# Hybrid encoder layer on one core: three products turned from by-feature to by-token blocks of 512 columns, with their results turned through DRAM

## The chip, the cores and the metric

The kernel runs on one core of a Trainium2 chip. The metric is device time in microseconds (us) of one execution; the kernel before takes 2039.56 us, the median of three runs (2039.33 to 2039.59). Profiles come from one execution recorded by the hardware profiler. A core has TensorE (matrix products, PE in the views; its weight loads are PEld), VectorE (DVE), ScalarE (ACT), GpSimd (POOL) and SyncE (SP). Here SP and POOL mostly issue DMAs.

## The reference

One layer works on x of 256 tokens by 2048 features, in float32:

```python
h = rms_norm(x, ffn1_norm);  x = x + 0.5 * swiglu_ffn(h, ffn1_w_in, ffn1_w_out)
h = rms_norm(x, mix_norm)
a_val, a_gate, g_u, g_v = split(h @ w_mix_in)
ya = silu(layer_norm(causal_conv31(a_val * sigmoid(a_gate))))
yb = gelu(g_u) * (masked W_s @ layer_norm(gelu(g_v)) + b)
x = x + concat(rms_norm(ya), rms_norm(yb)) @ w_mix_out
q = rms_norm(x, xattn_norm) @ w_q;  k, v = split(rms_norm(mem, mem_norm) @ w_kv)
x = x + softmax(q k^T / sqrt(512)) v @ w_o          # 4 heads of 512 features
h = rms_norm(x, ffn2_norm);  x = x + 0.5 * swiglu_ffn(h, ffn2_w_in, ffn2_w_out)
return rms_norm(x, final_norm)
```

The feed-forward's hidden width is 5632, the memory has 256 tokens.

## The kernel before

**Precision.** Every operand of a product is kept as a high and a low half in TensorE's fp32r type, and a product is the sum of high x high, high x low and low x high. Weights come from DRAM as float32 in pieces of 512 KB, which `weights` (L134) loads on SP's queue, casts on ScalarE (high half, L141) and subtracts on VectorE (low half, L142). Four raw pieces (`wraw`) and three pieces of halves (`whl`) are held at a time.

**Two forms of a product.** `gemm_t` (L191, by way of `ahead` and `product_part`) works by feature: the weights of 128 features are TensorE's stationary operand, and x streams past, both halves of it at once for the weights' high half (512 columns, L171), x's high half alone for the weights' low half (256 columns, L179). The result has features on the partitions and tokens in the columns, as the next product wants it. `gemm_n` (L209) works by token: x's halves are the stationary operand, and 512 weight columns stream past in three matmuls per k and half of the tokens (L220, L221, L222). Its result has tokens on the partitions. `sent` (L356) turns such a result into the layout by feature: VectorE transposes it in squares of 32 (L359), POOL's queue writes it to DRAM (L361) and reads it back in four pieces (L364). The columns of the weights are laid out beforehand so that the squares land in order (`by_blocks`).

**Order of work.** The program is written for a builder that orders each engine's instructions by its own forecast of the timeline, within the data's dependences; `tc.issue_after` adds an edge. `beside` hands out small pieces of other work after each weight piece, `between` is a list of pieces that `gemm_n` takes one by one. The two feed-forwards are different: `Line` (L419) keeps a list of items, each with its weight piece, and fixes the order on every engine (L497). Item s may be followed by preparation of up to six items ahead at the start. Its buffers for halves (`places`) and raw weights (`raws`) are lists too.

**The stages around the change.** The mixers' stage (L1172) makes the conv and gMLP inputs, the memory's keys and values by token. Then come

- the mixers' output projection (L1448 to L1459): by feature, 16 blocks; the first three begin with their upper half of k, and each block ends in `residual` (L330): two VectorE adds into xT from PSUM (L333), the halves of the next normalized x (`gained`, L318, on ScalarE L320 and VectorE L321) and its squares (L291);
- the queries (L1470), by feature, four blocks a head, each joined, and split into halves;
- per head, `probabilities` (L1482: scores, softmax), `turned` (L1507: transposes on TensorE) and `attend` (L1521: four results of 128 features, each split into `o_hl`);
- attention's output projection (L1550 to L1583), by feature, with parts of its first blocks put between heads 2 and 3, and `residual` behind each block;
- the second `FeedForward` (L1586), built after that. Its `begin` (L817) has 16 items of one k each, with the turning of x for the last residual (`x_turn`, L1594, after items 1 to 8), its two stores (`x_leaves`, after items 6 and 10), its squares' sums, and the sums of halves for a seven-product scheme (`sides`, L618) after items 3, 6, 9 and 12.

PSUM has eight banks: six named acc, two named aux. Large SBUF areas S0, S1, S2 are passed from stage to stage.

Of the kernel before, what the change touches and what calls it, by code (L numbers as in the profile page):

```python
# [14 lines left out]
ALU = mybir.AluOpType  # L15
# [47 lines left out]

LAST = ((256, True, False), (512, True, False), (256, False, False), (512, False, False), (512, False, True))
# [30 lines left out]
def layer(ctx: ExitStack, tc: tile.TileContext, a: dict):  # L95
# [19 lines left out]
    newest = [None]  # L115

# [17 lines left out]
    def weights(src, kk, n, hl=None):  # L134
# [6 lines left out]
        nc.scalar.copy(out=hl[:, 0, :size], in_=raw[:, :size])  # L141
# [67 lines left out]
    def gemm_n(w, x_hl, per=0.0, between=None, after=4, acc=None, ks=None, step=2):  # L209

        acc = acc or [ps.tile([P, 2, 256], F32, name="acc").rearrange("p a b -> p (a b)") for _ in range(2)]
        nk = w.shape[1]
        for k0 in ks or range(0, nk, 2):
            kk = min(2, nk - k0)
            hi, lo = weights(w[:, k0:k0 + kk, :], kk, 512)
            for k in range(kk):
                x = x_hl(k0 + k)
                for t in range(2):
                    s = slice(t * P, (t + 1) * P)
                    nc.tensor.matmul(acc[t], lhsT=x[:, 0, s], rhs=hi[:, k], start=k0 + k == 0, stop=False)  # L220
                    nc.tensor.matmul(acc[t], lhsT=x[:, 0, s], rhs=lo[:, k], start=False, stop=False)  # L221
                    nc.tensor.matmul(acc[t], lhsT=x[:, 1, s], rhs=hi[:, k], start=False, stop=k0 + k == nk - 1)  # L222
# [107 lines left out]
    def residual(acc, f, scale, x_hl, norm, ss):  # L330
# [6 lines left out]
        square_into(ss, xT[:, f], f == 0)  # L337

# [187 lines left out]
    class FeedForward:  # L526
# [6 lines left out]
        def __init__(self, stack, tags, name, x_hl, gain, w_in, w_out, patterns, sums, steps, out_s, late):  # L533
# [25 lines left out]
            spare = big.tile([P, 8192], F32, name="spare", tag=tags[2])  # L559
            raws = [spare[:, i * 1024:(i + 1) * 1024] for i in range(6)]  # L560
            self.u = [spare[:, 6144 + i * 512:6144 + (i + 1) * 512] for i in range(4)]
            self.raws_summed = [raws.pop() for _ in range(2)]
# [8 lines left out]
            self.in_low, self.in_high = self.fixed(lows), self.fixed(highs)  # L571
            self.in_spare = self.fixed(raws)
            self.line.places.extend(self.in_ring + self.in_low + self.in_high)
# [243 lines left out]
        def begin(self, before, after, scales):  # L817
# [19 lines left out]
            for i in range(len(self.spairs)):  # L837
# [4 lines left out]
                for q, part in enumerate(parts):  # L842
                    items[3 * i + q + 3].post.append(part)
# [135 lines left out]
    with ExitStack() as stack:  # L979
# [3 lines left out]
        )  # L983
        line = ff.line
# [187 lines left out]
    with ExitStack() as stack:  # L1172
        with tc.tile_pool(name="mix", bufs=1) as pool:
# [274 lines left out]
            ws = [a["w_mix_out"][f] for f in range(3)]  # L1448
            accs = ahead(ws, lambda k: y_hl[:, k], per=1.3, ks=[(8, 8)], end=False)
# [4 lines left out]
            for f in range(KD):  # L1454
                if f < 3:
                    acc = gemm_t(a["w_mix_out"][f], lambda k: y_hl[:, k], acc=accs[f], ks=[(0, 8)])
                else:
                    acc = gemm_t(a["w_mix_out"][f], lambda k: y_hl[:, k])
                residual(acc, f, 1.0, x_hl, "xattn_norm", ss)  # L1459


        with tc.tile_pool(name="attn", bufs=1) as pool:
            o_hl = big.tile([P, KD, 2, T], F32R, name="o_hl", tag="S2")

            def query(q_hl, d, acc):
                t = ev.tile([P, T], F32, name="tg")
                joined(acc, t)
                split(q_hl[:, d, 0], q_hl[:, d, 1], t)

            def queries(h, between=None):  # L1470
                q_hl = pool.tile([P, KH, 2, T], F32R, name="q_hl", bufs=2)
                if h == 0:
                    accs = ahead([a["w_q"][d] for d in range(2)], lambda k: x_hl[:, k])
                    for d in range(2):
                        query(q_hl, d, accs[d])
                for d in range(2 if h == 0 else 0, KH):
                    query(q_hl, d, gemm_t(a["w_q"][h * KH + d], lambda k: x_hl[:, k]))
                    if d == KH - 2 and between is not None:
                        between()
                return q_hl  # L1480

# [393 lines left out]
```

## Time and profile before

| | us |
|---|---|
| median of three runs | 2039.56 |
| profiled execution | 2040.7 |
| its span, first to last instruction | 2038.5 |
| TensorE busy | 2027.2 |
| VectorE busy | 1796.6 |
| ScalarE busy | 1244.7 |
| mixers' output projection, on TensorE | from 1051.7 |
| first matmul of attention's output projection | 1245.7 |
| DMA moved | 488.50 MB |

A row of groups reads: line, engine, operation, output<-inputs, shapes, count, then busy time and mean duration. A row of a stretch (`A:B`) gives the length, then for PE, PEld, DVE, ACT and POOL the busy time with the number of instructions, then TensorE's granted clock, the busy share of the DMA engines and GB/s. A row of waits gives total, number and longest in us. In the view of one line or tile, durations are minimum/median/maximum in ns, followed by the first and the last start in us. Matmuls overlap, so a matmul's own duration says less than the spacing of starts.

### The profile page before, as it was taken

The page shows a single profiled execution, that of the slowest core. Times are in us where ns is not written, and L with a number is a line of the kernel's source. Part 1 is how long each engine was busy: PE and PEld are TensorE (multiplying, and loading weights), DVE is VectorE, ACT ScalarE, POOL GpSimd, SP SyncE. Part 2 cuts the span into 40 slices and gives each one's busy share as a digit, 9 for nine tenths or more (in the row PEclk, how much of TensorE's full clock was granted, in tenths as well). Part 3 has the DMA queues.
Part 4 walks back from the last instruction along what each step waited for, and adds up shares of the span by engine and source line. Part 5 has one row for each costly group of instructions (what it writes and reads, how often), then busy time and mean ns, then how long its engine had stood idle before and what let it go on. Part 6 is the DMA issues. An engine that isn't in the chain of part 4 may idle for free.

```text
span 2038.5 us, 26768 instructions
## 1 busy us (share of the span) xinstructions
PE 2027.2 (99%) x9388; PEld 1690.5 (83%) x9388; DVE 1796.6 (88%) x2538; ACT 1244.7 (61%) x1609; POOL 123.6 (6%) x180
## 2 busy tenths in 40 slices
PE   9999999999999999999999999999999999999998
PEld 7888888888888887888888899888888888888886
DVE  7999999989898979999897666788999999988997
ACT  7666666656665654545675455556667666655555
POOL 0000000000110011011000000000001000000002
PEclk9999999999999999999999999999999999999999
DMA  9889898989676577677665543687888898896665
GB/s 352 272 259 275 269 277 260 273 250 289 213 262 233 194 260 224 210 227 230 203 196 195 186 157 116 204 290 259 262 263 268 269 276 268 233 300 203 207 226 177
DMA packets 146071, 488.50 MB, mean 240 GB/s; under 512 B 17040, under 2 KB 28944, under 8 KB 145296
## 3 DMA queue, kind: packets, MB, share of 16 engines
q1 hardware_dynamic: 130032, 432.64, 62.2%
q0 software_dynamic: 15328, 53.49, 13.1%
q8 instruction: 73, 1.20, 0.2%
q10 hardware_dynamic: 576, 0.66, 0.1%
q14 instruction: 62, 0.51, 0.1%
HBM read 465.76 MB, written 20.97 MB: 239 GB/s over the span
## 4 chain that ended last, share of the span: by engine, by line
PE 89%; DVE 4%; DMA 3%; ACT 2%; issue 1%; POOL 0%; SPq 0%; ACTq 0%; DVEq 0%; POOLq 0%
PE acc L388 13%; PE acc L387 13%; PE acc L390 13%; PE acc L171 9%; PE acc L375 6%; PE acc L374 6%; PE acc L376 6%; PE acc L179 5%; PE acc L221 4%; PE acc L222 4%; PE acc L220 4%; PE aux L375 2%; PE aux L374 2%; PE aux L376 2%; DVE hl L459 1%
## 5 line engine op out<-in xcount | busy, mean ns | idle before, releaser
L141 ACT CAST hl<-raw 128x1024 fp32r<-128x1024 f32 (+1 forms) x228 | 235.2, 1035 | 223.1 <-PE acc L222 85.3
L142 DVE TENSOR_TENSOR hl<-raw,hl 128x1024 fp32r<-128x1024 f32 (+1 forms) x228 | 273.7, 1203 | 78.0 <-ACT hl L141 77.6
L484 ACT CAST hl<-raw 128x1024 fp32r<-128x1024 f32 (+1 forms) x132 | 129.8, 995 | 62.7 <-DVE raw L679 22.7
L459 DVE TENSOR_TENSOR hl<-raw,hl 128x1024 fp32r<-128x1024 f32 (+1 forms) x132 | 151.5, 1154 | 15.9 <-ACT hl L484 13.6
L221 PE MATMUL acc<-hl,m_hl 128*128 128x512 f32 x256 | 100.6, 393 | 0.0
L221 PE MATMUL acc<-hl,x_hl 128*128 128x512 f32 x256 | 100.4, 392 | 0.0
L222 PE MATMUL acc<-hl,x_hl 128*128 128x512 f32 x256 | 99.8, 390 | 0.0
L222 PE MATMUL acc<-hl,m_hl 128*128 128x512 f32 x256 | 99.7, 390 | 0.0
L220 PE MATMUL acc<-hl,x_hl 128*128 128x512 f32 x256 | 89.7, 391 | 1.0 <-ACT hl L141 1.0
L220 PE MATMUL acc<-hl,m_hl 128*128 128x512 f32 x256 | 90.1, 391 | 0.0
L484 ACT CAST hl<-sums 128x1024 fp32r<-128x1024 f32 x50 | 52.6, 1052 | 60.4 <-DVE sums L676 55.0
L615 POOL DMA_DIRECT2D hl_s<-in_ffn_w_in x36 | 31.6, 877 | 870.9 <-ACT hl_s L613 453.0
L388 PE MATMUL acc<-hl,x_hl 128*128 128x512 f32 x192 | 75.1, 391 | 0.2 <-DVE hl L150 0.2
L387 PE MATMUL acc<-hl,x_hl 128*128 128x512 f32 x192 | 75.1, 391 | 0.1
L388 PE MATMUL acc<-more,x_hl 128*128 128x512 f32 x184 | 71.7, 390 | 0.0
L387 PE MATMUL acc<-more,x_hl 128*128 128x512 f32 x184 | 71.7, 389 | 0.0
L484 ACT CAST hl<-raws_out 128x1024 fp32r<-128x1024 f32 (+1 forms) x53 | 51.9, 985 | 27.8 <-PE acc L390 10.0
L459 DVE TENSOR_TENSOR hl<-raws_out,hl 128x1024 fp32r<-128x1024 f32 (+1 forms) x53 | 61.2, 1159 | 8.1 <-ACT hl L484 7.1
L613 ACT ACTIVATE more<-spare 128x1024 fp32r<-128x1024 f32 x36 | 38.1, 1059 | 44.9 <-PE acc L388 44.9
L171 PE MATMUL acc<-o_hl,hl 128*128 128x512 f32 x256 | 62.8, 392 | 0.0
L171 PE MATMUL acc<-x_hl,hl 128*128 128x512 f32 x256 | 62.1, 392 | 0.0
L171 PE MATMUL acc<-y_hl,hl 128*128 128x512 f32 x256 | 61.8, 391 | 0.0
(654 smaller groups left out, 6190.7 us busy)
## 6 DMA issues: line engine op xcount, KB each, us to landing
spare<-in_ffn_w_in SPq DMA_DIRECT2D x208, 512.0 KB, 6.8
raw<-in_ffn_w_in SPq DMA_DIRECT2D x143, 512.0 KB, 6.8
raw<-in_ffn_w_out SPq DMA_DIRECT2D x90, 512.0 KB, 5.3
raws_out<-in_ffn_w_out SPq DMA_DIRECT2D x68, 512.0 KB, 4.9
hl_s<-in_ffn_w_in POOLq DMA_DIRECT2D x36, 512.0 KB, 7.1
more<-in_ffn_w_in POOLq DMA_DIRECT2D x36, 512.0 KB, 7.4
raw<-in_w_mix_vg SPq DMA_DIRECT2D x32, 512.0 KB, 4.8
raw<-in_w_k SPq DMA_DIRECT2D x32, 512.0 KB, 4.3
```

The source lines that it names most:

```text
L141: nc.scalar.copy(out=hl[:, 0, :size], in_=raw[:, :size])
L142: newest[0] = nc.vector.tensor_tensor(out=hl[:, 1, :size], in0=raw[:, :size], in1=hl[:, 0, :size].bitcast(F32), op=ALU.subtract)
L171: done = nc.tensor.matmul(acc, lhsT=hi[:, k], rhs=xs[k], start=first and k == 0, stop=last and k == kk - 1, skip_group_check=True,)
L220: nc.tensor.matmul(acc[t], lhsT=x[:, 0, s], rhs=hi[:, k], start=k0 + k == 0, stop=False)
L221: nc.tensor.matmul(acc[t], lhsT=x[:, 0, s], rhs=lo[:, k], start=False, stop=False)
L222: nc.tensor.matmul(acc[t], lhsT=x[:, 1, s], rhs=hi[:, k], start=False, stop=k0 + k == nk - 1)
L374: nc.tensor.matmul(acc, lhsT=x[0], rhs=hi, start=first, stop=False)
L387: nc.tensor.matmul(acc[t][g], lhsT=x[:, 0, s], rhs=hi[:, cols[g]], start=(t, g) in first, stop=False)
L388: nc.tensor.matmul(acc[t][g], lhsT=x[:, 0, s], rhs=lo[:, cols[g]], start=False, stop=False)
L390: done = nc.tensor.matmul(acc[t][g], lhsT=x[:, 1, s], rhs=hi[:, cols[g]], start=False, stop=last)
L459: nc.vector.tensor_tensor(out=hl[:, 1, :n], in0=item.raw[:, :n], in1=hl[:, 0, :n].bitcast(F32), op=ALU.subtract)
L484: nc.scalar.copy(out=item.hl[:, 0, :item.n], in_=item.raw[:, :item.n])
```

## The change

1. The mixers' output projection, the queries and attention's output projection are computed with `gemm_n`: four blocks of 512 features instead of sixteen of 128. The weights w_mix_out, w_q and w_o are laid out for it.
2. `by_tokens` copies a block's two token halves out of PSUM on ScalarE and calls `sent`. For the residuals, `arriving` gives two pieces of work per block: the first adds the returned block to xT (two VectorE adds) and prepares two features of x, the second the other two. They are taken after weight pieces of the following block or product: block 3 of the mixers' projection during the queries of head 0, block 3 of attention's during items 4 and 5 of the second feed-forward.
3. The queries return as a flat tile; `halves_by_feature` splits it with the keys just ahead of the scores, after the newest weight cast. The split of the values is put after it too.
4. The mixers' projection begins with two blocks' upper half of k (three before, of a quarter of the width). In attention's end, two blocks of 512 columns are begun between the heads instead of four of 128.
5. The second `FeedForward` is built ahead of the last part of attention's output projection, whose blocks return into its tiles `whole`. The part of its set-up that needs area S2 (`spared`) comes after. In `begin`, `sides` move to items 0, 1, 2 and 9, `x_turn` to items 6 to 13, its stores to 11 and 15, the sums to 10.

```diff
+    def by_tokens(name, acc, flat, back, scales=None):
+        o = flat.rearrange("p (q t n) -> p q t n", q=4, t=2)
+        for t in range(2):
+            nc.scalar.copy(out=o[:, :, t], in_=by_q(acc[t]))
+        sent(name, flat, back)
+
+    def arriving(f, flat, x_hl, norm, ss):
+        z = flat.rearrange("p (i t k a) -> p i t k a", i=4, t=2, k=4)
+        def add():
+            for t in range(2):
+                d = xT[:, f:f + 4, t * P:(t + 1) * P].rearrange("p k (i a) -> p k i a", i=4)
+                nc.vector.tensor_tensor(out=d, in0=d, in1=z[:, :, t].rearrange("p i k a -> p k i a"), op=ALU.add)
+        def one(k):
+            gained(x_hl, k, xT[:, k], col(norm, k))
+            square_into(ss, xT[:, k], k == 0)
+        return [lambda: (add(), one(f), one(f + 1)), lambda: (one(f + 2), one(f + 3))]
...
-            ws = [a["w_mix_out"][f] for f in range(3)]
-            accs = ahead(ws, lambda k: y_hl[:, k], per=1.3, ks=[(8, 8)], end=False)
+            accs = [gemm_n(a["w_mix_out"][n], y_of, per=1.3, ks=range(8, KD, 2), first=8, last=-1) for n in range(2)]
             finish()
...
-            for f in range(KD):
-                if f < 3:
-                    acc = gemm_t(a["w_mix_out"][f], lambda k: y_hl[:, k], acc=accs[f], ks=[(0, 8)])
-                else:
-                    acc = gemm_t(a["w_mix_out"][f], lambda k: y_hl[:, k])
-                residual(acc, f, 1.0, x_hl, "xattn_norm", ss)
+            arrivals = []
+            for n in range(4):
+                if n < 2:
+                    acc = gemm_n(a["w_mix_out"][n], y_of, acc=accs[n], between=arrivals, after=0, ks=range(0, 8, 2), first=-1, last=7)
+                else:
+                    acc = gemm_n(a["w_mix_out"][n], y_of, between=arrivals, after=8)
...
+                by_tokens(f"x_away{n}", acc, flat, flat)
+                arrivals += arriving(4 * n, flat, x_hl, "xattn_norm", ss)
...
-            q = queries(0)
+            q = queries(0, arrivals, 8, 2)
...
-            begun(0, 0, 8)
-            begun(1, 0, 4)
+            begun(0, 0, 6)
             turn_now(2)()
             with tc.issue_after(state["turned"].ins):
-                done = begun(1, 4, 4)
+                done = begun(0, 6, 2)
             with tc.issue_after(done.ins):
                 state["p"] = probabilities(3, q_next)
                 attend(2, *state["v"])
-            begun(2, 0, 8)
+            begun(1, 0, 8)
             turn_now(3)()
             with tc.issue_after(state["turned"].ins):
                 begun(0, 8, 4)
-                begun(1, 8, 4)
-                done = begun(2, 8, 4)
+                done = begun(1, 8, 4)
             with tc.issue_after(done.ins):
                 attend(3, *state["v"])
...
+        for n in range(4):
+            acc = gemm_n(
+                a["w_o"][n], o_of, acc=accs[n] if n < 2 else None, ks=range(12, KD, 2) if n < 2 else None,
+                between=arrivals, after=8,
+            )
+            flat = ff.whole[n // 2][:, n % 2]
+            by_tokens(f"o_away_{n}", acc, flat, flat)
+            arrivals += arriving(4 * n, flat, x_hl, "ffn2_norm", ss)
+        ff.spared()
...
-        after = {k: [lambda k=k: x_turn(k - 1)] for k in range(1, 9)}
-        after[6].append(x_leaves(0))
-        after[10] = [x_leaves(1)]
-        after[9] = [x_sums]
+        after = {k: [lambda k=k: x_turn(k - 6)] for k in range(6, 14)}
+        after[4], after[5] = [arrivals[0]], [arrivals[1]]
+        after[11].append(x_leaves(0))
+        after[15] = [x_leaves(1)]
+        after[10].append(x_sums)
```

More of the change, by code (lines that the diff above doesn't have):

```diff
@@ L115, in layer @@
     newest = [None]
+    newest_matmul = [None]
+    newest_copy = [None]
     def put(cost, *parts):
@@ L140, in weights @@
             hl = whl.tile([P, 2, 1024], F32R, name="hl")
-        nc.scalar.copy(out=hl[:, 0, :size], in_=raw[:, :size])
+        newest_copy[0] = nc.scalar.copy(out=hl[:, 0, :size], in_=raw[:, :size])
         newest[0] = nc.vector.tensor_tensor(
@@ L207, in ahead, with gemm_n @@
         return accs
-    def gemm_n(w, x_hl, per=0.0, between=None, after=4, acc=None, ks=None, step=2):
+    def gemm_n(w, x_hl, per=0.0, between=None, after=4, acc=None, ks=None, step=2, first=None, last=None):
         acc = acc or [ps.tile([P, 2, 256], F32, name="acc").rearrange("p a b -> p (a b)") for _ in range(2)]
         nk = w.shape[1]
+        first, last = 0 if first is None else first, nk - 1 if last is None else last
         for k0 in ks or range(0, nk, 2):
@@ L815, in block, with begin @@
             return parts, b, made
-        def begin(self, before, after, scales):
+        def begin(self, before, after, scales, sides_at=(3, 6, 9, 12)):
             acc = []
@@ L842, in begin @@
                 for q, part in enumerate(parts):
-                    items[3 * i + q + 3].post.append(part)
+                    items[sides_at[i] + q].post.append(part)
             self.sides_left = later_sides
@@ L1453, in layer @@
             ss = st.tile([P, T], F32, name="ss", bufs=2)
-            for f in range(KD):
-                if f < 3:
-                    acc = gemm_t(a["w_mix_out"][f], lambda k: y_hl[:, k], acc=accs[f], ks=[(0, 8)])
-                else:
-                    acc = gemm_t(a["w_mix_out"][f], lambda k: y_hl[:, k])
-                residual(acc, f, 1.0, x_hl, "xattn_norm", ss)
-        with tc.tile_pool(name="attn", bufs=1) as pool:
[L1463 to L1480, printed above, removed]
-            def probabilities(h, q_hl):
-                k_hl = pool.tile([P, KH, 2, M], F32R, name="k_hl")
-                z = kT[:, h].rearrange("p (i t k a) -> p i t k a", i=4, t=2, k=4)
@@ new lines, in layer, with queries, halves_by_feature @@
+        with tc.tile_pool(name="attn", bufs=1) as pool:
+            def queries(h, between=None, after=8, step=8):
+                acc = gemm_n(a["w_q"][h], lambda k: x_hl[:, k], between=between, after=after, step=step)
+                flat = pool.tile([P, 1024], F32, name="q", bufs=2)
+                by_tokens(f"q_away{h}", acc, flat, flat)
+                return flat
+            def halves_by_feature(name, flat):
+                hl = pool.tile([P, KH, 2, T], F32R, name=name)
+                z = flat.rearrange("p (i t k a) -> p i t k a", i=4, t=2, k=4)
@@ L1568, in layer @@
                 begun(0, 8, 4)
-                begun(1, 8, 4)
-                done = begun(2, 8, 4)
+                done = begun(1, 8, 4)
             with tc.issue_after(done.ins):
                 attend(3, *state["v"])
-            accs.append(ps.tile([P, 2, 256], F32, name="acc"))
-            begun(3, 0, 8)
-            x_hl = gained_tile("S1")
-            ss = st.tile([P, T], F32, name="ss", bufs=2)
-            for f in range(KD):
-                if f < 4:
-                    acc = gemm_t(a["w_o"][f], o_of, acc=accs[f], ks=[(12, 4)] if f < 3 else [(8, 8)])
-                else:
-                    acc = gemm_t(a["w_o"][f], o_of)
-                residual(acc, f, 1.0, x_hl, "ffn2_norm", ss)
     with ExitStack() as stack:
+        x_hl = gained_tile("S1")
+        ss = st.tile([P, T], F32, name="ss", bufs=2)
         ff = FeedForward(
```

49 lines of the change are left out of this document (33 added, 16 removed).

## The prediction, made before the change was run

> **What bounds the kernel now.** I read the page first, for the engine that is full and for the chain that ended last.
>
> ```profile
> span 2038.5 us, 26768 instructions
> PE 2027.2 (99%) x9388; PEld 1690.5 (83%) x9388; DVE 1796.6 (88%) x2538; ACT 1244.7 (61%) x1609; POOL 123.6 (6%) x180
> PE 89%; DVE 4%; DMA 3%; ACT 2%; issue 1%; POOL 0%; SPq 0%; ACTq 0%; DVEq 0%; POOLq 0%
> ```
>
> TensorE is busy for 99% of the span and carries 89% of the chain. Then the table by stretches: keys of the memory and gMLP input, output projection of the mixers, queries with the first heads, and attention's output projection with the last heads.
>
> ```profile
> core 0: us, PE busy (x) PEld busy (x) DVE busy (x) ACT busy (x) POOL busy (x), PEclk, DMA share, GB/s
> 870.00:962.00 92.00, 92.00 (x413) 76.43 (x412) 85.78 (x150) 42.51 (x46) 11.06 (x20) 1.00 0.77 232
> 1051.00:1140.00 89.00, 89.00 (x513) 78.66 (x512) 67.38 (x102) 48.91 (x70) 0.00 (x0) 1.00 0.57 190
> 1140.00:1245.00 105.00, 105.00 (x644) 94.30 (x643) 66.26 (x111) 55.09 (x95) 0.00 (x0) 1.00 0.48 160
> 1245.00:1344.00 99.00, 99.00 (x598) 88.61 (x598) 71.75 (x124) 52.01 (x87) 0.00 (x0) 1.00 0.52 168
> ```
>
> The last three rows are the stages that the change rewrites, 1051 to 1344 us. TensorE has no idle time there, at a granted clock of 1.00, while VectorE is busy for only 63 to 76% and ScalarE for about half. So only two things can move the time here: what the products themselves cost on TensorE, and waits that the new form brings to it. The waits of TensorE in the whole span:
>
> ```profile
> PE aux L249 <- DVE ones L246: 1.1, 1, 1.1
> PE acc L220 <- ACT hl L141: 1.0, 3, 0.4
> PE acc L388 <- DVE hl L150: 0.2, 1, 0.2
> PE acc L388 <- DVE hl L459: 0.2, 1, 0.2
> ```
>
> None belongs to L171 or L179, the lines of the old products. There is no wait that the change could remove.
>
> **The price of a product in each form.** Old form, by feature, from the chain of waits:
>
> ```profile
> 1077.86 3.65 PE acc L171 x16
> 1081.51 1.91 PE acc L179 x16
> ...
> 1094.56 3.65 PE acc L171 x16
> ```
>
> Each of the 16 blocks of 128 features takes, per k, one matmul of 512 columns (L171: both halves of x at once) and one of 256 (L179). From 1077.86 to 1094.56 lie three blocks, so one takes 5.567 us, and a product 16 x 5.567 = 89.1 us. The 512 wide matmul costs 3.65/16 = 228 ns, the 256 wide 1.91/16 = 119 ns: more than half.
>
> New form, by token; L220 is the first of its three matmuls:
>
> ```profile
> L220 PE MATMUL acc<-hl,x_hl x60: 388/389/390, 919.2 to 959.3; 128*128 128x512 f32 x60
> ```
>
> Three matmuls of 512 columns take (959.3 - 919.2)/59 = 0.680 us. The duration of 389 ns is no price, because matmuls overlap; the spacing is. A product has 4 blocks x 16 k x 2 token halves = 128 such triples: 87.0 us. The saving is 89.1 - 87.0 = 2.0 us a product. Three products are rewritten (mixers, queries, attention's result): **-6.1 us**. The times of rows are given to 0.1 us, so one product's saving is good to about 0.3 us.
>
> [...]
>
> The scores and the attention itself keep their matmuls. Weights arrive in the same 512 KB pieces, 32 a product, with the same ScalarE and VectorE work each.
>
> **The evacuation and its trip through DRAM.** Nothing of this shape runs in the three stages before, but the key and gMLP stages do the same, block for block: two ScalarE copies, a VectorE transpose, a write by POOL's queue and four reads.
>
> ```profile
> 940.76 0.39 PE L222 MATMUL acc<-hl,x_hl 128*128 128x512 f32 x1
> 940.84 1.27 ACT L1411 ACTIVATE o<-acc,r_t 128x512 f32<-128x512 f32 x2
> 942.14 1.24 DVE L359 STREAM_TRANSPOSE o<-o 128x1024 f32<-128x1024 f32 x1 [0.17 <-ACT o L1411]
> 943.78 0.56 POOL L361 DMA_DIRECT2D u_away<-o  x1 [16.00 <-DVE half L1217]
> 947.10 2.21 POOL L364 DMA_DIRECT2D o<-u_away  x4 [2.76 <-DMA u_away<-o]
> DMA to landing us min/median/max: 2.9/5.7/7.2
> ```
>
> The block's last matmul is issued at 940.76, so its successor at about 940.99. The last of the four reads is issued at 947.10 + 2.21 - 0.55 = 948.76 and takes 7.2 us at most: landed at about 956.0. **15.0 us** pass from the end of a block to its data, 12.2 of them in DMA. The row 870 to 962 above shows that TensorE stays full beside four such trips (x20 on POOL: five DMAs each) with VectorE at 93%, so a trip costs nothing where nobody waits for it.
>
> In work off the path: per block the new form has one transpose (1.24) and two adds of 512 (0.68, below) on VectorE in place of eight adds out of PSUM, and two copies more on ScalarE. Twelve trips move 12 x 1 MB. With VectorE at 63 to 76% and a DMA share near 0.5 this hides; were the cover gone, VectorE would have to reach the 93% of the row 870 to 962, and even that row costs TensorE nothing. I take 0.
>
> **First end that can stick out: mixers to queries.** The queries run by k from 0, and x by feature 12 to 15 comes from the last block of the mixers. It is due after 6 pairs of k. A pair is 4 triples, 2.72 us, so the cover is 16.3 us. The data land at 15.0; then follow the add of L1073's shape and the splitting:
>
> ```profile
> L1073 DVE TENSOR_TENSOR xT<-xT,o x4: 683/684/684, 661.0 to 679.9; 128x512 f32<-128x512 f32 x4
> L320 ACT ACTIVATE x_hl<-xT,pv x31: 499/500/516, 1065.8 to 1340.0; 128x256 fp32r<-128x256 f32 x31
> L321 DVE SCALAR_TENSOR_TENSOR x_hl<-xT,pv,x_hl x31: 472/478/483, 1067.4 to 1341.3; 128x256 fp32r<-128x256 f32 x31
> ```
>
> 15.0 + 2 x 0.68 + 0.50 + 0.48 = 17.4 us; features 13 to 15 follow faster than TensorE takes them. That is 1.1 us late. Bounds: 0 if the trip is 1.1 us shorter in a stage with less DMA traffic, and 4 us if one weight subtraction of 1.2 us and one cast get in ahead on each engine. I take **+1.2**, the sum of the rows.
>
> [...]
>
> **Second: fewer PSUM banks in attention's end.** Two blocks of the output projection now hold four of the six banks while head 3 is attended, where three held three. attend() has four results; the third now needs the bank of the first.
>
> ```profile
> L149 ACT CAST o_hl<-acc x16: 372/372/393, 1213.0 to 1268.0; 128x256 fp32r<-128x256 f32 x16
> L150 DVE TENSOR_TENSOR o_hl<-acc,o_hl x16: 412/417/425, 1214.3 to 1268.4; 128x256 fp32r<-128x256 f32 x16
> ```
>
> One result is six matmuls of 256 columns, 6 x 0.119 = 0.72 us. The first is emptied 0.72 + 0.37 + 0.42 and about 0.3 of hand-over later, at 1.8 us; the third would begin at 1.43. I take **+0.5**, between 0 and 1.7 (one weight operation of 1.2 us ahead).
>
> **Third: adds that wait in VectorE's queue.** arriving() stands in the order of work before weight subtractions. If the data are late, the add blocks VectorE, and behind it stand the subtractions that TensorE needs next. The builder orders instructions by its own forecast; the trace shows both sides of that.
>
> ```profile
> 735.35 2.23 POOL L364 DMA_DIRECT2D o<-g_away  x4 [2.50 <-DMA g_away<-o]
> 735.60 2.93 ACT L141 CAST hl<-raw 128x1024 fp32r<-128x1024 f32 x3
> 742.93 0.71 ACT L1239 COPY pad<-o 128x256 f32<-128x256 f32 x2
> ```
>
> ```profile
> ACT pad L1239 <- DMA o<-g_away: 9.5, 3, 3.5
> ```
>
> The copy written right behind the trip was put behind later casts, so the written order is not kept blindly; yet three of four such copies still waited, 9.5 us in all, 3.2 each. Three blocks of weights are held, so TensorE has one or two pairs (2.7 to 5.4 us) in hand and most of such a wait is swallowed. I take **+0.6** for seven such places, between 0 and 13 (the rival below). The queries have 21.8 us of cover before their head is scored. Head 3's have two attentions, 8 k of the output projection and little else, about 17 us against 15.0 plus two splits: 0.1, in the same 0.6.
>
> **Setting up the second feed-forward ahead.** Its first loads wait for the same buffers as before, and TensorE had no wait at that seam, so it gains nothing. The last block's add now comes at its items 4 and 5, and x's turn for the residual moves from items 1 to 8 to items 6 to 13, with its store on SP's queue. VectorE can stand at that add until 15.0 us; six items, 16 us of TensorE, are made ahead by then. The store's first half is now posted after item 11, not 6, and its tile is overwritten by group 0's result after item 15, 4 x 2.72 = 10.9 us later:
>
> ```profile
> 1374.00:1384.00 10.00, 10.00 (x46) 8.28 (x45) 8.44 (x14) 8.31 (x11) 0.00 (x0) 1.00 0.64 256
> 1384.00:1394.00 10.00, 10.00 (x45) 8.23 (x44) 5.21 (x8) 6.15 (x8) 0.93 (x1) 1.00 0.18 29
> ```
>
> ```profile
> DMA to landing us min/median/max: 6.6/7.0/7.4
> ```
>
> The two stores took 6.6 and 7.4 us, so 10.9 covers them unless SP's loads ahead of them wait for over 3 us. VectorE idles 6.3 of these 20 us, and the moved work (two adds, four splits with their squares) is about 5 us. I take 0, between 0 and 3.
>
> **Sum.** -6.1 + 1.2 + 0.5 + 0.6 = -3.8 us. The profiled execution took 2040.7 us, its span 2038.5 and 2.2 around it; it becomes 2036.9. The median of 2039.56 lies 1.1 below the profiled execution, so the forecast is **2035.8 us**.
>
> **Rivals.**
> - *Everything is hidden.* The three waits vanish: 2039.56 - 6.1 = 2033.5, to about 2035. For it: the full row 870 to 962. Against: the 1.1 us worked out at the first seam, from rows with little spread.
> - *VectorE's queue starves TensorE (slower).* The adds are put too early, each of seven waits 3.2 us and adds 1.4, and only one pair of 2.72 us is in hand: 1.9 x 7 = 13 us lost, 2039.6 - 6.1 + 1.7 + 13 = 2048. It decides from the point where a wait and its adds exceed one pair. For it: the 3.2 us above, and that blocks 0 of the first and third product are asked for one pair after they are sent. Against: ScalarE's waits of that kind cost TensorE 1.0 us in all (the L220 row).
> - *The narrow matmuls are no dearer by the column.* Both forms stream the same columns (256 x 768 = 384 x 512), so if the 119 ns come from something else in those stages, the gain is 0 and the waits remain: 2042. [...] Against: 119 and 228 ns hold over whole stages.
>
> **How the numbers follow.** A difference of 0.2%, 4.1 us, is about what a measurement of this kernel can tell from no change. Forecast 0.40, its own range 2034.5 to 2039; all hidden 0.32; starved 0.17; no gain 0.11. Faster by over 0.2% means under 2035.5: the hidden case and a quarter of the forecast's, 0.42. Slower: the starved case, 0.17. The rest, 0.41, is within. The range begins a little under the hidden case, 2033.3, for the 0.3 us by which a saving can be off; it ends where the upper bounds of the seam, the banks and the feed-forward would bring the sum with the third wait at 0.6: 2039.6 - 6.1 + 4 + 1.7 + 3 + 0.6 = 2042.8, so 2043. Outside lies the starved case.
>
> **What would show it.** Right: the rows of L220 to L222 replace L171 and L179 in all three stages at 0.227 us a matmul; about 289 us from the first output matmul to the second feed-forward, against 293; a gap of about 1 us on TensorE near 16 us into the queries, and one of half a microsecond in head 3's attention. Wrong: spacing over 0.227, VectorE's adds waiting on o or x_away with TensorE's gaps behind them, or a feed-forward whose VectorE falls behind after item 5.

## The result and the profile after

The changed kernel takes **2051.31 us** (median of 4 runs, 2049.72 to 2056.08) against 2039.57 us (4 runs, 2039.33 to 2039.78): a ratio of 1.0061, 95% interval [1.0044, 1.0079]. It is 11.7 us slower. The forecast, 2035.8 us, and its range, 2033.3 to 2043.0, both missed it.

The profiled execution took 2049.72 us. Its page, first the span, then the engines, then the chain of waits:

```profile
span 2047.9 us, 26059 instructions
PE 2027.9 (99%) x9004; PEld 1673.6 (82%) x9004; DVE 1785.4 (87%) x2474; ACT 1250.3 (61%) x1605; POOL 157.2 (8%) x240
PE 38%; issue 3%; DMA 3%; DVE 1%; POOL 1%; ACT 1%; SPq 0%; ACTq 0%; DVEq 0%; POOLq 0%
```

TensorE issues 384 matmuls fewer, as the new form wants (128 x 3 per product instead of 512), yet its busy time is the same. The chain no longer lies on TensorE all the way: followed back from the end it leaves TensorE for the trips through DRAM (o_away, x_away), and there it stops, so its shares add up to less than half. The table by stretches, with the same columns and stretches as before:

```profile
870.00:962.00 92.00, 92.00 (x411) 76.36 (x410) 85.64 (x148) 44.32 (x49) 11.09 (x20) 1.00 0.77 231
1051.00:1140.00 89.00, 85.64 (x370) 70.16 (x369) 53.32 (x64) 44.43 (x64) 8.32 (x15) 0.98 0.69 213
1140.00:1245.00 105.00, 104.00 (x515) 87.72 (x514) 69.20 (x96) 59.09 (x89) 11.76 (x21) 1.00 0.71 216
1245.00:1344.00 99.00, 97.22 (x464) 81.35 (x464) 58.44 (x88) 48.03 (x76) 10.55 (x19) 0.98 0.63 196
```

Ahead of the change nothing differs (first row). In the three rewritten stages TensorE has idle time for the first time, and the granted clock falls to 0.98 in two of them. VectorE is not short of time: it is busy for 53 of 89 us, less than before. Who waits for whom is in the waits of TensorE (total, number, longest):

```profile
PE acc L226 <- DVE hl L146: 6.6, 3, 3.2
PE acc L225 <- ACT x_hl L327: 1.0, 1, 1.0
PE acc L404 <- DVE hl_l L488: 1.0, 2, 0.8
PE acc L417 <- DVE hl L488: 0.8, 2, 0.6
```

L226 is the second matmul of a triple, the first that needs the weights' low half; L146 is VectorE's subtraction that makes it. (In the changed kernel L225 to L227 are the triple, L404 and L417 matmuls of the second feed-forward, L360 the arriving add, L388 the transpose, L390 and L393 the write and the reads of a trip.) The weights are late from VectorE, and VectorE's own waits from 1050 to 1420 us say why (the rows at L360):

```profile
DVE xT L360 <- DMA z<-o_away: 10.3, 2, 5.3
DVE xT L360 <- DMA o<-x_away: 9.8, 3, 7.0
DVE xT L360 <- DMA h<-o_away: 5.6, 1, 5.6
DVE xT L360 <- DMA last_o<-x_away: 2.2, 1, 2.2
```

It stood 28 us at the adds of returning blocks. The dearest case, block 2 of the mixers' projection, in VectorE's timeline (start, duration, and in brackets the idle time before with its releaser):

```profile
1115.89 1.25 DVE L388 STREAM_TRANSPOSE o<-o 128x1024 f32<-128x1024 f32 x1 [0.20 <-ACT o L350]
1117.06 1.18 DVE L146 TENSOR_TENSOR hl<-raw,hl 128x1024 fp32r<-128x1024 f32 x1
1119.08 1.23 DVE L146 TENSOR_TENSOR hl<-raw,hl 128x1024 fp32r<-128x1024 f32 x1 [0.83 <-ACT hl L145]
1121.80 1.23 DVE L146 TENSOR_TENSOR hl<-raw,hl 128x1024 fp32r<-128x1024 f32 x1 [1.50 <-ACT hl L145]
1124.52 1.23 DVE L146 TENSOR_TENSOR hl<-raw,hl 128x1024 fp32r<-128x1024 f32 x1 [1.50 <-ACT hl L145]
1132.76 1.29 DVE L360 TENSOR_TENSOR xT<-xT,o 128x512 f32<-128x512 f32 x2 [7.01 <-DMA o<-x_away]
1133.97 1.22 DVE L146 TENSOR_TENSOR hl<-raw,hl 128x1024 fp32r<-128x1024 f32 x1
```

The subtractions come every 2.72 us, one pair of k; the next was due at 1127.24 and came at 1133.97. Only four stand between the block's transpose and its add, so VectorE is at the add 8.6 us after the transpose (1117.14 to 1125.75). The chain of waits over the same place (start, duration, what) shows the trip itself:

```profile
1117.54 7.00 DMA x_away<-o
...
1126.60 6.04 DMA o<-x_away
1132.76 0.10 DVE xT L360
```

The write took 7.00 us, the last read 6.04. And TensorE's timeline shows what it cost:

```profile
1129.13 0.39 PE L226 MATMUL acc<-hl,y_hl 128*128 128x512 f32 x1
...
1131.17 0.39 PE L227 MATMUL acc<-hl,y_hl 128*128 128x512 f32 x1
1131.39 0.61 PE L225 MATMUL acc<-hl,y_hl 128*128 128x512 f32 x2
1135.24 0.80 PE L226 MATMUL acc<-hl,y_hl 128*128 128x512 f32 x1 [3.23 <-DVE hl L146]
...
1136.26 0.63 PE L226 MATMUL acc<-hl,y_hl 128*128 128x512 f32 x1
1136.69 0.63 PE L227 MATMUL acc<-hl,y_hl 128*128 128x512 f32 x1
```

Before the stall, from 1129.13 to 1131.17, nine matmuls follow at 0.227 us. Then TensorE stands for 3.4 us, and behind that the matmuls come at 0.43 us, not 0.227, until 1138.4.

The whole account, from the starts of all matmuls between 1045 and 1425 us: gaps of 3.4 and 0.4 us at block 2 of the mixers, 1.2 at the seam into the queries (1158 us), 1.9 at attention's blocks 0 and 1 (1316), 1.7 and 0.8 at its block 2 (1344 and 1349), 2.1 in the second feed-forward (1401 to 1404), together 11.5 us; and three stretches of 6, 7 and 7 matmuls at 0.43 us instead of 0.227, 4.0 us. 11.5 + 4.0 - 6.1 saved = +9.4 us, and the span grew by 2047.9 - 2038.5 = 9.4.

### The profile page after: what moved, and what is told of

It reads as the page before. It is cut to its first block, busy times and chain, and to the rows that moved or that the text cites. A ratio compares the mean times of both kernels' runs of the same rounds, so it can differ in the third digit from the quotient of the medians.

```text
span 2047.9 us, 26059 instructions
## 1 busy us (share of the span) xinstructions
PE 2027.9 (99%) x9004; PEld 1673.6 (82%) x9004; DVE 1785.4 (87%) x2474; ACT 1250.3 (61%) x1605; POOL 157.2 (8%) x240
## 2 busy tenths in 40 slices
DMA packets 149525, 501.05 MB, mean 245 GB/s; under 512 B 17936, under 2 KB 29840, under 8 KB 148752
## 5 line engine op out<-in xcount | busy, mean ns | idle before, releaser
L145 ACT CAST hl<-raw 128x1024 fp32r<-128x1024 f32 x224 | 235.3, 1052 | 234.4 <-PE acc L227 176.5
L146 DVE TENSOR_TENSOR hl<-raw,hl 128x1024 fp32r<-128x1024 f32 x224 | 273.1, 1221 | 96.0 <-ACT hl L145 95.6
L513 ACT CAST hl<-raw 128x1024 fp32r<-128x1024 f32 (+1 forms) x132 | 129.7, 994 | 57.4 <-DVE raw L711 22.4
L488 DVE TENSOR_TENSOR hl<-raw,hl 128x1024 fp32r<-128x1024 f32 (+1 forms) x132 | 151.6, 1155 | 14.0 <-ACT hl L513 11.7
L226 PE MATMUL acc<-hl,x_hl 128*128 128x512 f32 x384 | 150.3, 391 | 0.0
L227 PE MATMUL acc<-hl,x_hl 128*128 128x512 f32 x384 | 149.1, 390 | 0.0
L225 PE MATMUL acc<-hl,x_hl 128*128 128x512 f32 x384 | 134.9, 390 | 1.0 <-ACT x_hl L327 1.0
L226 PE MATMUL acc<-hl,m_hl 128*128 128x512 f32 x256 | 100.6, 393 | 0.0
L227 PE MATMUL acc<-hl,m_hl 128*128 128x512 f32 x256 | 99.6, 389 | 0.0
L225 PE MATMUL acc<-hl,m_hl 128*128 128x512 f32 x256 | 90.0, 391 | 0.0
L225 PEld LDWEIGHTS acc<-hl,x_hl 128*128 128x128 f32 x384 | 72.0, 188 | 16.4 <-ACT x_hl L327 1.4
L227 PEld LDWEIGHTS acc<-hl,x_hl 128*128 128x128 f32 x384 | 72.1, 188 | 14.8 <-DVE x_hl L328 0.2
L226 PEld LDWEIGHTS acc<-hl,x_hl 128*128 128x128 f32 x384 | 72.1, 188 | 14.7
L417 PE MATMUL acc<-hl,x_hl 128*128 128x512 f32 x192 | 75.1, 391 | 0.8 <-DVE hl L488 0.6
L416 PE MATMUL acc<-hl,x_hl 128*128 128x512 f32 x192 | 74.9, 390 | 0.0
L417 PE MATMUL acc<-more,x_hl 128*128 128x512 f32 x184 | 71.6, 389 | 0.0
```

Of the source, the lines that this page charges most:

```text
L145: newest_copy[0] = nc.scalar.copy(out=hl[:, 0, :size], in_=raw[:, :size])
L146: newest[0] = nc.vector.tensor_tensor(out=hl[:, 1, :size], in0=raw[:, :size], in1=hl[:, 0, :size].bitcast(F32), op=ALU.subtract)
L227: newest_matmul[0] = nc.tensor.matmul(acc[t], lhsT=x[:, 1, s], rhs=hi[:, k], start=False, stop=k0 + k == last)
L416: nc.tensor.matmul(acc[t][g], lhsT=x[:, 0, s], rhs=hi[:, cols[g]], start=(t, g) in first, stop=False)
L417: nc.tensor.matmul(acc[t][g], lhsT=x[:, 0, s], rhs=lo[:, cols[g]], start=False, stop=False)
L488: nc.vector.tensor_tensor(out=hl[:, 1, :n], in0=item.raw[:, :n], in1=hl[:, 0, :n].bitcast(F32), op=ALU.subtract)
```

## The experiments

**Theory 1**: VectorE takes its instructions in order (above, the subtraction due at 1127.24 us comes at 1133.97, behind the add). It stands at an add that waits for a trip, and the weights' subtractions behind it come too late for TensorE. **Theory 2**: the added traffic slows the weights' loads. **Theory 3**: the added copies, transposes and adds are too much work for the engines. Each kernel is compared with the kernel before on the same chip, which took 2040 to 2041 us there.

### Without the trips, and with the trips but nobody waiting

First, the two residual results are copied and transposed but not sent; the adds take the block where it lies. The turn of the two results is left out.

```diff
-    def sent(name, flat, back, q=None):
+    def sent(name, flat, back, q=None, trip=True):
         nc.vector.transpose(out=flat, in_=flat)
+        if not trip:
+            return
...
-        sent(name, flat, back)
+        sent(name, flat, back, trip=name[0] == "q")
```

> The changed kernel without the trips through DRAM of the mixers' and of attention's result: their blocks are copied and transposed but neither written nor read back, so the adds take untransposed data (the turn of the two results is what is left out); the queries keep their trips. Theory 1 (waits for the trips): nothing waits for a trip in the two products, and the whole saving of 6.1 us shows: 2033 to 2036. Theory 2 (traffic): the traffic of eight of twelve trips is gone, 2033 to 2038 as well. Theory 3 (added work on the engines): all of it but the trips' descriptors is still there, 2046 or above.

Measured: 2034.59 us (7 runs, 2033.75 to 2035.32) against 2040.25, ratio 0.9973 [0.9962, 0.9984]. All the copies, transposes and adds are in it: theory 3 is out. To part the wait from the traffic, the second kernel keeps every write and read but lets the reads land in another place in DRAM, so that no add waits for them; the turn of the two results is left out here too:

```diff
+        if not trip:
+            back = dram.tile([P, flat.shape[-1]], F32, name=name + "_aside")
         z = back.rearrange("p (i n) -> p i n", i=4)
```

> The changed kernel with all of its writes and reads of the two results, but the reads land in another place in DRAM and the adds take the untransposed blocks in SBUF, as in the run without the trips (the turn of the two results is what is left out): the traffic is at least that of the change, nothing waits for it. Theory 1 (VectorE standing at an add until a trip is back): as without the trips, 2034.6, within 1.5 us. Theory 2 (traffic that slows the weights' loads): it stays near the changed kernel, 2046 to 2052.

Measured: 2034.04 us (6 runs, 2033.22 to 2036.53) against 2039.96, ratio 0.9973 [0.9961, 0.9985]. Its DMA view names the same packets and bytes as that of the changed kernel (149525 and 501.05 MB):

```profile
DMA packets 149525, 501.05 MB, mean 247 GB/s; under 512 B 17936, under 2 KB 29840, under 8 KB 148752
```

Of the waits of TensorE for L146, 6.6 us in the changed kernel, only this one is there, and it lies ahead of the three stages; from 1040 to 1420 us TensorE waits for nobody:

```profile
PE acc L226 <- DVE hl L146: 0.4, 1, 0.4
```

The same traffic without anybody waiting cost nothing (2034.04 us, against 2034.59 without the two results' trips): theory 2 is out, and the whole loss is the wait. (These reads write into DRAM and not into SBUF; the last kernels below keep the reads as they were and lose nothing either.) Both kernels gain 5.7 to 5.9 us, with intervals from 3 to 8, which fits the 6.1 us of the matmul term.

### The queries alone; the mixers and the queries

Both undo the rest of the change: the other products go back to `gemm_t` and `residual`, the second feed-forward is set up as before.

```diff
-            accs = [None, None]
+            accs = [ps.tile([P, 2, 256], F32, name="acc") for _ in range(3)]
...
+                    acc = gemm_t(a["w_o"][f], o_of)
+                residual(acc, f, 1.0, x_hl, "ffn2_norm", ss)
```

> The kernel before with the queries alone by token; mixers' and attention's results and the second feed-forward as before. Theory 1: no residual add hangs on the queries' trips and no weights stand behind them, so the product's own 2.0 us show: about 2037.5 (2036.5 to 2038.5). Theories 2 and 3, a loss shared evenly by three products that each bring the same traffic and the same evictions: 2039.6 + 11.7 / 3 = 2043.5.

Measured: 2039.34 us (10 runs, 2038.95 to 2040.14) against 2040.25, ratio 0.9996 [0.9986, 1.0005]. Neither number was met. The trace has no wait at a trip, but it has one that none of the theories held, in the attention of a head:

```profile
PE aux L159 <- DVE p_hl L154: 0.9, 1, 0.9
PE acc L159 <- ACT p_hl L153: 0.8, 1, 0.8
```

There are two gaps of 1.0 and 1.1 us, at 1248 and 1250 us, together as long as what the queries were to save. The kernel before and the changed kernel have no such gap there. That it comes from queries by token beside an attention projection by feature, so that what stands between a head's softmax and its attention no longer fits, is argued and not shown. So this run says nothing against the queries' trips, and its gain can't be read from it alone.

> Mixers' result and queries by token; attention's result and the second feed-forward as before. Theory 1: two products' saving of 4.1 us against the stall at block 2's add (3.4 us and 1.7 us of half-speed matmuls behind it) and 1.2 us at the seam into the queries: 2039.6 - 4.1 + 5.1 + 1.2 = 2041.8 (2038 to 2043, the stall being one execution's). Theories 2 and 3: two thirds of the loss, 2047.

Measured: 2045.47 us (8 runs, 2041.70 to 2048.47) against 2040.25, ratio 1.0025 [1.0014, 1.0035]. That is above theory 1's range and below the 2047 of the others. In its trace stand 1.8 us at block 0 of the mixers, 2.7 at block 2, 3.1 at the seam with half-speed matmuls behind it (granted clock 0.98 from 1138 to 1240 us), and 2.1 us between softmax and attention. The places are theory 1's (and one of the run above), the sizes are not those of the changed kernel's one trace: there VectorE's longest wait at the first three adds is 7.0 us and the one at block 3's add 2.2, here they are 5.8 and 4.2.

### The adds later

`late` pins a block's two pieces behind the newest weight cast, and they are taken at a later k. The first hunks are the helper and the mixers, then come attention's projection and the second feed-forward.

```diff
+    def late(parts):
+        def go():
+            with tc.issue_after(newest[0].ins):
+                for part in parts:
+                    part()
+        return [go]
...
-                    acc = gemm_n(a["w_mix_out"][n], y_of, between=arrivals, after=8)
+                    acc = gemm_n(a["w_mix_out"][n], y_of, between=arrivals, after=14)
...
+                arrivals += late(parts) if n in (1, 2) else parts
...
-                between=arrivals, after=8,
+                between=arrivals if n > 1 else None, after=14 if n < 3 else 0, step=2 if n < 3 else 14,
...
-        after = {k: [lambda k=k: x_turn(k - 6)] for k in range(6, 14)}
-        after[4], after[5] = [arrivals[0]], [arrivals[1]]
+        after = {k: [lambda k=k: x_turn(2 * k - 16), lambda k=k: x_turn(2 * k - 15)] for k in range(8, 12)}
+        after[6], after[7] = [arrivals[0]], [arrivals[1]]
```

> The changed kernel whole, with its residual adds taken later in VectorE's queue: those of the mixers' blocks 1 and 2 and of attention's blocks 0, 1 and 2 behind more of the weights' subtractions, those of attention's block 3 at items 6 and 7 of the second feed-forward instead of 4 and 5; every transfer, cast and add stays. Theory 1 (VectorE stands at an add that waits for a trip through DRAM, and the weights' subtractions queued behind it starve TensorE): the stalls at 1131, 1316, 1344, 1349 and 1401 us of the changed kernel's trace go, some 5.1 + 3.8 + 1.7 + 0.8 + 4 us, and the time falls from 2051.3 to about 2036 (2034 to 2040). Theory 2 (the added traffic slows the weights' loads): the traffic is the same, 2047 or above. Theory 3 (the added evictions, transposes and adds are too much work for VectorE, ScalarE and GpSimd): the work is the same, 2047 or above.

Measured: 2041.28 us (10 runs, 2037.71 to 2044.64) against 2040.25, ratio 1.0005 [0.9995, 1.0015]. With every transfer and instruction kept, 10 us of the change's time are gone; 2034 to 2040 was hoped for. What is left of TensorE's waits:

```profile
PE acc L226 <- DVE hl L146: 3.8, 4, 1.5
PE acc L412 <- DVE hl_l L496: 0.8, 1, 0.8
PE acc L225 <- ACT x_hl L327: 0.7, 1, 0.7
```

The first row belongs to adds that still wait, above all block 0 of the mixers and attention's block 1:

```profile
1099.40 1.29 DVE L360 TENSOR_TENSOR xT<-xT,o 128x512 f32<-128x512 f32 x2 [2.98 <-DMA o<-x_away]
1318.39 1.29 DVE L360 TENSOR_TENSOR xT<-xT,h 128x512 f32<-128x512 f32 x2 [2.21 <-DMA h<-o_away]
```

The first of them was not moved. The second was, but its trip took 20 us from the transpose on. Of the other rows, L412 stands in the second feed-forward (1395 us) and L225 at the seam into the queries (1156 us). The three places by themselves, one of the three hunks each:

> The changed kernel with only the mixers' adds of blocks 1 and 2 later in VectorE's queue. Theory 1: the stall at 1131 us goes (3.4 us and 1.7 us of half-speed matmuls), the others stay: 2051.3 - 5.1 = 2046.2 (2044 to 2049, since block 0's add may stall in its place as it did with all adds later, 1.6 us). Theory 2: no change, 2051.

Measured: 2046.32 us (8 runs, 2045.16 to 2049.28) against 2039.96, ratio 1.0033 [1.0022, 1.0043].

> The changed kernel with only attention's adds of blocks 0, 1 and 2 later. Theory 1: the stalls at 1316 and 1344 us (1.9 us with 1.9 us at half speed behind it, and 1.7 us) give way to those that stood with all adds later (2.2 us at 1322 to 1327): 2051.3 - 5.5 + 2.2 = 2048 (2046 to 2050). Theory 2: no change, 2051.

Measured: 2047.20 us (5 runs, 2045.79 to 2049.56) against 2039.96, ratio 1.0038 [1.0024, 1.0053].

> The changed kernel with only attention's block 3 later: its adds at items 6 and 7 of the second feed-forward instead of 4 and 5, the turns of x two to an item from item 8 to 11. Theory 1: the stalls at 1401 to 1408 us (2.1 us and about 1.9 us at half speed) shrink as they did with all adds later (1.5 us): 2051.3 - 2.5 = 2049 (2046.5 to 2051). Its rival, that each stall only moves to the next block: no change, 2051.

Measured: 2048.06 us (4 runs, 2046.16 to 2052.79) against 2041.03, ratio 1.0039 [1.0024, 1.0055].

All three came out as theory 1 had them (2046.2, 2048 and 2049). Each place holds about a third of the loss: by the ratios, 1.0061 falls to 1.0033, 1.0038 and 1.0039, that is 5.7, 4.7 and 4.5 us. Their sum, 15 us, is more than the 11.4 us that all three together brought (1.0061 to 1.0005); each ratio is good to 2 to 4 us either way, which leaves room for both.

### Later still, and where it works

> All adds later still than in the first kernel that took them late: the mixers' block 0 at the start of block 2, block 1 in the middle of block 2, block 2 late in block 3; attention's blocks 0, 1 and 2 at the start, the middle and the end of block 3, its block 3 at items 6 and 7 of the second feed-forward, the turns of x one to an item from item 8. Theory 1: of the 6.2 us of stalls that were left the 1.6 us at 1100, the 2.2 us at 1322 and the 1.5 us at 1395 go, the seam into the queries (0.9 us) stays: 2041.3 - 5.3 = 2036 (2035 to 2038.5). Theory 2: no change against the first such kernel, 2041.

Measured: 2045.73 us (8 runs, 2043.68 to 2048.96) against 2039.96, ratio 1.0029 [1.0019, 1.0040]. The expectation fell: this is slower than the first kernel with late adds. Its trace shows why. Block 0 of the mixers was moved from the end of one block to "the start of the next", which on VectorE is the same place: its add stands at 1099.5 us, as before, and TensorE loses 1.9 us there. The later step in the program was not a later place on VectorE. Attention's adds are now all in block 3; block 2's stands there behind only five subtractions and waits for its trip again:

```profile
1343.67 1.29 DVE L360 TENSOR_TENSOR xT<-xT,z 128x512 f32<-128x512 f32 x2 [3.46 <-DMA z<-o_away]
```

The largest loss, however, is at the seam into the queries, which this kernel leaves as it was: 2.7 us at 1158 us, where 0.9 us had been expected. The mean granted clock of this execution is 0.997, against 0.999 in the two runs without waits for the trips.

So the last kernels place each add by counting the subtractions that VectorE's own order has between the block's transpose and its add: six or more for every block. For the seam, the last 4 of the 16 k of head 0's queries come after 2 steps (4 k) of head 1's.

```diff
+    acc = gemm_n(a["w_mix_out"][n], y_of, at={2: {8: [0], 14: [1]}, 3: {14: [2]}}[n])
...
-            q = queries(0, arrivals, 8, 2)
+            accs = [gemm_n(a["w_q"][0], lambda k: x_hl[:, k], ks=range(0, 12, 2), at={})]
+            accs.append(gemm_n(a["w_q"][1], lambda k: x_hl[:, k], ks=range(0, 4, 2), at={2: [3]}))
+            q = queries(0, acc=accs[0], ks=range(12, KD, 2))
...
+                at={2: {14: [0]}, 3: {6: [1], 14: [2]}}.get(n, {}),
...
-        after = {k: [lambda k=k: x_turn(k - 6)] for k in range(6, 14)}
-        after[4], after[5] = [arrivals[0]], [arrivals[1]]
+        after = {k: [lambda k=k: x_turn(k - 8)] for k in range(8, 16)}
+        after[6], after[7] = [parts[0]], [parts[1]]
```

`at` names, for each block and k, the blocks whose adds `gemm_n` takes there.

> All adds placed behind six or more of the weights' subtractions that follow the block's transpose in VectorE's queue, 13 to 16 us after the block leaves, and the last 4 features of the first head's queries taken after the first 2 steps of the second head's, so that the seam is covered by 21.7 us instead of 16.3; attention's block 3 at items 6 and 7, turns of x one to an item from item 8. Theory 1: no add waits longer than the subtractions' lead and the 5.9 us that two kernels without the waits have saved show: 2034 to 2037. Its rival, that each stall only moves on: 2041 to 2046 as with the adds later in two other ways.

Measured: 2035.24 us (7 runs, 2033.65 to 2036.25) against 2041.03, ratio **0.9971** [0.9960, 0.9982].

The second such kernel has the turns of x as in the kernel with all adds late:

```diff
-        after = {k: [lambda k=k: x_turn(k - 8)] for k in range(8, 16)}
+        after = {k: [lambda k=k: x_turn(2 * k - 16), lambda k=k: x_turn(2 * k - 15)] for k in range(8, 12)}
```

> The same kernel with the turns of x two to an item at items 8 to 11. Theory 1: within 1.5 us of it; the 1.5 us stall at 1395 us that stood with the turns two to an item may come back. The rival: 2041 to 2046.

Measured: 2034.74 us (5 runs, 2033.10 to 2035.46) against 2041.03, ratio **0.9969** [0.9956, 0.9981]. Both compute the whole layer and are faster than both kernels. In the stretches of the second one TensorE is full again, at a granted clock of 1.00:

```profile
1051.00:1140.00 89.00, 89.00 (x395) 73.71 (x394) 57.14 (x70) 47.91 (x68) 8.30 (x15) 1.00 0.74 228
1140.00:1245.00 105.00, 105.00 (x526) 89.24 (x525) 70.83 (x106) 59.54 (x91) 13.89 (x25) 1.00 0.70 218
1245.00:1344.00 99.00, 99.00 (x475) 83.15 (x474) 67.13 (x93) 55.28 (x87) 8.88 (x16) 1.00 0.65 204
```

And VectorE's timeline at the same block 2, six subtractions behind the transpose instead of four, the add (here L362) without a wait:

```profile
1116.53 1.25 DVE L400 STREAM_TRANSPOSE o<-o 128x1024 f32<-128x1024 f32 x1
...
1118.00 1.22 DVE L146 TENSOR_TENSOR hl<-raw,hl 128x1024 fp32r<-128x1024 f32 x1
...
1130.60 1.23 DVE L146 TENSOR_TENSOR hl<-raw,hl 128x1024 fp32r<-128x1024 f32 x1 [1.50 <-ACT hl L145]
1131.74 1.29 DVE L362 TENSOR_TENSOR xT<-xT,o 128x512 f32<-128x512 f32 x2
```

Over all eight returning blocks the count tells the two kernels apart. In the changed kernel four or five subtractions stand between transpose and add (ten at attention's last block), and seven of the eight adds wait, 1.1 to 7.0 us. In this second kernel with counted places it is six or more, and the longest wait is 0.4 us. Six is no fixed limit: with all adds late, attention's block 2 stood behind six and still waited 2.0 us.

The last run puts the change's own seam back into this kernel, all else equal:

```diff
-            q = queries(0, acc=accs[0], ks=range(12, KD, 2))
+            q = queries(0, parts, 8, 2)
```

> The kernel with all adds behind six or more subtractions and the turns two to an item (2034.7 us), with the seam into the queries as the change made it: the first head's queries whole, block 3's adds inside them. The prediction priced this seam at 1.2 us of late features (17.4 us back against 16.3 us of cover); the traces with the seam in them stand there 0.9 to 2.7 us. Theory 1: 2034.7 + 0.9 to 2.7, about 2036.2 (2035.5 to 2038), all of the difference at the seam. Its rival, that the seam is hidden once the other stalls are gone: 2034.7.

Measured: 2037.64 us (11 runs, 2035.08 to 2041.20) against 2040.39, ratio 0.9988 [0.9979, 0.9997]. The seam is not hidden: its price is 2.9 us by the medians (2037.64 - 2034.74), 3.9 by the ratios (0.9988 to 0.9969), whose intervals allow 1 to 7. In its trace one wait of TensorE is left in the three stages, at 1153 us, and VectorE's 2.80 us at block 3's add ahead of it:

```profile
PE acc L225 <- ACT x_hl L329: 1.6, 1, 1.6
```

```profile
1149.38 1.23 DVE L146 TENSOR_TENSOR hl<-raw,hl 128x1024 fp32r<-128x1024 f32 x1 [1.50 <-ACT hl L145]
1153.40 1.29 DVE L362 TENSOR_TENSOR xT<-xT,last_o 128x512 f32<-128x512 f32 x2 [2.80 <-DMA last_o<-x_away]
```

The spread goes with it: 6.1 us over 11 runs, 2.4 and 2.6 us over 5 and 7 runs without the seam.

## Why the prediction was wrong

- **The saving of 6.1 us: right.** The spacing is 0.227 us, and without the waits the gain is 5.7 to 6.3 us in four kernels. The rival by which narrow matmuls are no dearer is out: the intervals of these kernels begin at 3 us.
- **The trip costs nothing where nobody waits: right.** The run with the reads put aside shows it with all of the traffic (2034.04 us, against 2034.59 without the two results' trips).
- **"Adds that wait in VectorE's queue ... I take +0.6 for seven such places": this step failed.** It is the mechanism of the rival with a starved TensorE, which stood there with 0.17 and 2048 us. Without the seam's 2.2 us the adds waited 26 us. Some 10 us of that reached TensorE (11.5 less the seam's 1.2), and with 4.0 us at half speed they cost about 14 us, not 0.6. Two parts of the step were wrong. First, the 3.2 us came from a row of another stage; the trip's own 15.0 us were never set against the place of the add in VectorE's queue. In the program the add follows five pairs of the next block (`after=8`), 13.6 us. But VectorE prepares weights ahead of TensorE. In the trace the add stands behind the subtraction of the sixth pair, and VectorE is there 11.2 us after the block's copy began (1114.59 to 1125.75), while TensorE begins that pair only at 1128.67. Against its 15.0 us the prediction would have had 3.8 us of wait there, more than the pair in hand. Second, "most of such a wait is swallowed" took for a share what is a fixed time. ScalarE's waits at g_away were 2.8 to 3.5 us long, and the weight cast behind each came only 1.7 to 2.5 us late, less than one pair of 2.72 us. Here 3.3 us of the 6.7 us delay were swallowed, one pair and a bit; the rest was lost whole.
- **The trip of 15.0 us: too short.** It came from a single trip, which took 13.9 us from the transpose to the last landing (942.14 to 956.0). The eight trips of the changed kernel's residuals took 13.6 to 19.1 us, five of them over 15. At block 2 of the mixers the write took 7.00 us against 2.9, and the data were back 18.1 us after the copy began. Attention's blocks 0 and 1 leave 2.5 us apart, so their trips overlap; they took 17.7 and 18.1 us. The trace before held a warning that was not used: where the first feed-forward's result is turned (`o_away` at 589 to 615 us), the second of two writes took 9.7 us, and 19.8 us passed from its issue to the last landing, against 12.2 in the row that was taken.
- **The first seam, +1.2 us: right in place and mechanism, low in size.** The changed kernel's trace has 1.2 us there, the other traces with this seam 0.9 to 3.1, the 3.1 with half-speed matmuls behind it (granted clock 0.98 from 1138 to 1240 us). Over the runs the term is worth about 3 us (1 to 7 by the intervals); its bounds were 0 to 4.
- **Fewer PSUM banks, +0.5 us: not seen.** In the attention of head 3 the matmuls lose about 0.2 us.
- **The second feed-forward, 0 with bounds 0 to 3: the slack did not take it up.** VectorE stood 4.9 us at the add of block 3, and the moved work came together at 1401 us, a stall of 2.1 us and 1.4 us at half speed: 3.5 us, beyond the bound. With the adds two items later and the turns of x moved with them it nearly goes; which of the two does it was not parted. Setting the feed-forward up ahead costs nothing that shows: the last kernels keep it.

The sum lacked one term, the half speed behind a stall (4.0 us), and had one that was far too small. That one decided, because the waits at adds are all of one kind: seven of the eight stuck out, by 1.1 to 7.0 us.

## What to carry to other kernels

Put an instruction that waits for a transfer, in the queue of an engine that also feeds TensorE, behind as much of that engine's own work as the transfer lasts: here adds behind four or five subtractions waited up to 7.0 us, in the second kernel with six or more up to 0.4. Count the place in the engine's order, not in the program: VectorE, which prepares ahead, reached block 2's add 11.2 us after the block's copy began, where the program's five pairs are 13.6 us. Price such a wait against the longest time that the trace has for such a transfer, not against one row (the trace before has a write of 9.7 us beside the one of 2.9), and against the lead alone. A trip through DRAM that was covered cost nothing here (2034.04 us with all of the traffic, 2034.59 without the two results' trips).

## What was not expected of the hardware

**Half speed behind a stall.** A gap on TensorE cost more than its length. By the stretches of the changed kernel, the granted clock behind two of its stalls and after:

```profile
1135.80:1138.40 2.60, 2.60 (x8) 1.99 (x7) 2.60 (x6) 2.60 (x6) 0.00 (x0) 0.50 0.66 194
1139.00:1145.00 6.00, 6.00 (x28) 4.98 (x27) 4.48 (x5) 3.25 (x5) 0.13 (x1) 1.00 0.77 240
1319.70:1322.70 3.00, 3.00 (x8) 2.30 (x7) 3.00 (x6) 3.00 (x6) 0.00 (x0) 0.50 0.49 162
```

The changed kernel's trace has three such stretches from the mixers to the second feed-forward, and in each the granted clock is 0.50 for about 3.4 us: from 1135.2 to 1138.6 us, with the gap of 3.4 us at block 2 of the mixers ahead of it; from 1319.5 to 1322.9, with the 1.9 us at attention's blocks 0 and 1; and from 1404.8 to 1408.2, with the 2.1 us in the second feed-forward, which are three gaps of 0.4, 0.8 and 1.0 us. Each begins 2.8 to 3.6 us after its gap began (the first of the three, in the feed-forward). The six or seven matmuls that lie whole within one cost 1.2 to 1.4 us, 4.0 us in all. Behind the gaps of 1.2 us at 1158 us and of 1.7 and 0.8 us at 1344 and 1349 us the granted clock was 1.00 (1155 to 1165 and 1346 to 1352 us). What decides which gap is followed by half speed is not shown.

**The same trip, the same stage, different times.** In the changed kernel's trace the four blocks' writes of x_away by POOL's queue took 3.5, 3.7, 7.0 and 3.8 us from issue to landing, the reads 3.9 to 6.6 us. In the run with the reads put aside the median of the first three writes is 5.2 us, against 3.7. What sets it was not tried. It may be why the changed kernel's four runs spread over 6.4 us, against 0.5 us for the four of the kernel before beside them; with one trace for each kernel this is not shown, and on the other chips the kernel before itself spread over 3 to 5 us in 12 to 26 runs.
